# Storing the SwiGLU intermediate as two ready halves instead of splitting it where it is loaded

## The chip, the cores and the metric

The kernel runs on one core of a Trainium2 chip. The metric is the device time of one execution in microseconds, lower is better. The kernel is built by a tile framework: the program is written as Python calls on tiles, and a scheduler fixes the order in which each engine's queue gets its instructions.

## The reference, cut to what matters

Two layers, each a mixer and a SwiGLU channel mixer in sandwich norm, over 1024 tokens of width 1024 in float32. The change is in the two channel mixers (D_FF = 2816):

```
def sandwich(x, g_pre, g_post, fn):
    return x + rmsnorm(fn(rmsnorm(x, g_pre)), g_post)

def swiglu(h, w_gate, w_up, w_down):
    return (jax.nn.silu(h @ w_gate) * (h @ w_up)) @ w_down
```

## The kernel before

**Products in three parts.** Each float32 operand of a matmul is split into a rounded half hi (fp32r) and a remainder lo = x - hi. One product is three matmuls (`mm3`, L114): hi·hi, hi·lo and lo·hi, the fourth being left out. An operand is thus made ready by a cast (ScalarE) and a subtraction (VectorE or GpSimd).

**Seven products for eight.** The class `Ffn` computes both matrix products by a Strassen-Winograd scheme on 2x2 blocks: 7 products and a number of block sums.

**The up stage** (`up`, `pair`, L1168) has 11 iterations. Each makes seven products b1, b2, b5, b6, b3, b7, b4 of 24 matmuls of 512 columns, 168 in an iteration. The weights come in by SyncE (SP) as `raw` of 512 KB, ScalarE casts `wh` (L1121), GpSimd subtracts `wl` (L1123). VectorE adds the products out of PSUM (L1163, L1172), `emit` (L1141) applies silu on ScalarE (L1144) and multiplies by the up branch on VectorE (L1145), GpSimd makes four of the block sums in `store` (L1178). The seven blocks of h that an iteration makes, of 128 x 512 or 256 KB each, are stored to a DRAM buffer `h_s` (L1147, L1179).

**The down stage** (`down`, L1229) makes 42 products in passes over two (once one) of the 11 column blocks. `hraw` (L1244) loads a block pair of h (`hr`, 512 KB, L1246), `hx` casts it to `hh` (ScalarE, L1252) and subtracts `hl` (VectorE, L1253), each of 128 x 1024; four buffers of `hr`, `hh` and `hl`. The products go to banks named `psd`, in two loops over token blocks, `wide` and `slim`, and VectorE adds them to the accumulators `acc` (L1271). Block differences of the weights are made by `minus` (L1242). `end` runs the sandwich norm (L162 to L173) on finished rows; its loads are `r`, `gpost`, `gpre`.

**What else runs there.** In the up stage of layer 0, from `mid` on, the tables of the S5 layer are prepared by many small VectorE operations (`s5_prep`, from L583); they are independent of the FFN and run between its operations.

**Order.** All DMAs go through SP's queue in order, and each waits for the one eight places before it, since eight semaphores take turns. Every engine's queue is in order, so a waiting instruction holds all behind it. The split weights `wh` and `wl` go round a ring of three buffers, and of five between `K.more` and `K.less`; in layer 0's up stage the ring has three, in layer 1's five.

## Time and profile before

| | |
|---|---|
| median of 3 runs | 2328.96 us (2328.18 to 2329.32) |
| profiled execution | 2332.52 us, its span 2330.1 us, mean granted TensorE clock 0.968 |
| layer 0: up, down | about 493 to 961 us, 972 to 1195 us |
| layer 1: up, down | about 1627 to 2081 us, 2086 to 2318 us |

The profiled execution is 3.6 us above the median. Times in the rows are of that execution, counted from the span's start. "Idle before" and "releaser" tell how long an engine waited and what ended it; DMA share is the mean busy share of the 16 DMA engines.

### The profile page before, as it was taken

How to read it: one execution, taken by the hardware profiler on the slowest of the kernel's cores; microseconds unless marked ns; L12 is line 12 of the kernel's file. 1: busy time of each engine (PE TensorE's matmuls, PEld its weight loads, DVE VectorE, ACT ScalarE, POOL GpSimd, SP SyncE). 2: the span in 40 equal slices, each digit the busy share in tenths (PEclk: the TensorE clock that was granted, in tenths of full speed). 3: DMA queues.
4: the chain of work that ended last, by engine and by line, in shares of the span. 5: the costliest groups of instructions: out<-in, count | busy, mean ns of one | idle time of the engine just before them, and what ended most of it. 6: DMA issues, size and time to landing. Idle time of an engine off the chain costs nothing.

```text
span 2330.1 us, 27167 instructions
## 1 busy us (share of the span) xinstructions
PE 2157.9 (93%) x9684; PEld 1746.3 (75%) x9684; DVE 1594.9 (68%) x2175; ACT 945.2 (41%) x1413; POOL 1265.7 (54%) x740
## 2 busy tenths in 40 slices
PE   7999889898999999899969888999899999989987
PEld 5887677676788878687758767876688888878866
DVE  6859567689856865477884578656964444447788
ACT  5554555453222332333344346654532322234332
POOL 4997202134665556776644455421575656577674
PEclk9999999899999999899979999999999999999999
DMA  5234683243332343644542674324332323255354
GB/s 204 71 109 140 167 206 112 76 168 107 107 117 100 123 136 104 221 140 134 173 160 80 193 232 141 113 97 160 119 131 72 133 73 131 73 178 185 112 167 149
DMA packets 150662, 315.32 MB, mean 135 GB/s; under 512 B 20224, under 2 KB 43904, under 8 KB 150528
## 3 DMA queue, kind: packets, MB, share of 16 engines
q1 hardware_dynamic: 150528, 313.60, 41.4%
q8 instruction: 76, 1.25, 0.2%
q14 instruction: 58, 0.48, 0.1%
HBM read 214.39 MB, written 96.01 MB: 133 GB/s over the span
## 4 chain that ended last, share of the span: by engine, by line
PE 68%; DVE 16%; DMA 6%; issue 4%; ACT 3%; POOL 3%; SPq 0%; POOLq 0%; DVEq 0%; ACTq 0%
PE b L115 29%; PE psd L115 13%; PE psw L115 6%; PE psc L115 5%; PE psq L115 3%; PE po L115 2%; DVE hl L1253 2%; DVE acc L1271 2%; PE pss L1038 2%; PE trp L365 1%; POOL wl L1123 1%; DVE wt L1042 1%; PE pss L452 1%; DMA bm<-k_s 1%; PE psv L115 1%
## 5 line engine op out<-in xcount | busy, mean ns | idle before, releaser
L1123 POOL TENSOR_TENSOR wl<-raw,wh 128x1024 fp32r<-128x1024 f32 (+1 forms) x238 | 614.1, 2588 | 412.3 <-ACT wh L1121 399.7
L115 PE MATMUL b<-T,wh 128*128 128x512 f32 x1408 | 438.4, 392 | 2.2 <-DVE F L1172 2.2
L1121 ACT CAST wh<-raw 128x1024 fp32r<-128x1024 f32 (+1 forms) x238 | 241.9, 1023 | 433.0 <-PE b L115 251.7
L115 PE MATMUL b<-B,wh 128*128 128x512 f32 x1056 | 337.4, 400 | 15.0 <-DVE c L1163 10.5
L115 PEld LDWEIGHTS b<-T,wh 128*128 128x128 f32 x1408 | 263.8, 188 | 62.3 <-issue 2.8
L115 PE MATMUL b<-T,wl 128*128 128x512 f32 x704 | 276.4, 393 | 1.6 <-POOL wl L1123 1.6
L115 PE MATMUL psd<-wh,hh 128*128 128x512 f32 x616 | 240.6, 400 | 32.6 <-ACT hh L1252 18.9
L115 PEld LDWEIGHTS b<-B,wh 128*128 128x128 f32 x1056 | 203.0, 193 | 62.5 <-ACT B L1089 7.3
L115 PE MATMUL psd<-wl,hh 128*128 128x512 f32 x616 | 241.4, 396 | 0.0
L115 PE MATMUL psd<-wh,hl 128*128 128x512 f32 x616 | 235.2, 396 | 1.3 <-DVE hl L1253 1.3
L1271 DVE TENSOR_TENSOR acc<-acc,psd 128x512 f32<-128x512 f32 (+1 forms) x208 | 177.8, 884 | 60.1 <-PE psd L115 60.0
L115 PE MATMUL b<-B,wl 128*128 128x512 f32 x528 | 210.9, 400 | 3.6 <-POOL wl L1123 3.6
L115 PE MATMUL psw<-wh,jt 128*128 128x512 f32 x512 | 176.0, 410 | 16.0 <-ACT jt L488 9.3
L1172 DVE TENSOR_TENSOR p<-p,b 128x1024 f32<-128x1024 f32 (+1 forms) x88 | 83.5, 950 | 135.3 <-PE b L115 134.9
L1252 ACT CAST hh<-hr 128x1024 fp32r<-128x1024 f32 (+1 forms) x84 | 82.2, 979 | 223.8 <-PE psd L115 206.6
L115 PEld LDWEIGHTS psd<-wh,hh 128*128 128x128 f32 x616 | 117.2, 190 | 67.3 <-ACT hh L1252 23.9
L1253 DVE TENSOR_TENSOR hl<-hr,hh 128x1024 fp32r<-128x1024 f32 (+1 forms) x84 | 152.5, 1826 | 16.6 <-ACT hh L1252 16.6
L115 PEld LDWEIGHTS b<-T,wl 128*128 128x128 f32 x704 | 132.1, 188 | 32.7 <-POOL wl L1123 2.8
L91 POOL TENSOR_TENSOR wl<-raw,wh 128x1024 fp32r<-128x1024 f32 x48 | 122.2, 2558 | 58.4 <-ACT wh L89 58.4
L115 PEld LDWEIGHTS psd<-wh,hl 128*128 128x128 f32 x616 | 117.1, 190 | 28.9 <-DVE hl L1253 2.6
L115 PEld LDWEIGHTS psd<-wl,hh 128*128 128x128 f32 x616 | 117.5, 191 | 25.5
L1173 DVE TENSOR_TENSOR raw<-raw 128x1024 f32<-128x1024 f32 x66 | 106.7, 1617 | 41.3 <-POOL wl L1123 40.2
(386 smaller groups left out, 4314.4 us busy)
## 6 DMA issues: line engine op xcount, KB each, us to landing
raw<-in_l_gu_dram SPq DMA_DIRECT2D x96, 512.0 KB, 3.6
hr<-l_h_s SPq DMA_DIRECT2D x70, 512.0 KB, 4.1
raw<-in_l_dn_dram SPq DMA_DIRECT2D x48, 512.0 KB, 3.8
l_h_s<-F SPq DMA_DIRECT2D x66, 256.0 KB, 2.3
raw<-in_w_in_dram SPq DMA_DIRECT2D x27, 512.0 KB, 3.5
l_h_s<-c SPq DMA_DIRECT2D x44, 256.0 KB, 2.1
l_h_s<-p SPq DMA_DIRECT2D x44, 256.0 KB, 2.6
raw<-in_l_w_out_dram SPq DMA_DIRECT2D x16, 512.0 KB, 4.2
```

The source lines that it names most:

```text
L91: nc.gpsimd.tensor_tensor(lo, raw, hi.bitcast(F32), op=ALU.subtract)
L115: mm = lambda *t, **k: self.nc.tensor.matmul(*t, skip_group_check=go, **k)
L365: nc.tensor.transpose(tr[:, jj * P:(jj + 1) * P], Wt[:, offs[jj] + i * P:offs[jj] + (i + 1) * P], self.ident)
L452: nc.tensor.matmul(ps[:, b0:b0 + bw], Q[c][v][:, j * P:(j + 1) * P], M[c][:, b0:b0 + bw], start=v == 0, stop=v == 1)
L1038: nc.tensor.matmul(ps[:, ks], a[:, js], b[:, ks], start=first, stop=last)
L1121: nc.scalar.copy(hi[:, 0:n], r[:, 0:n])
L1123: nc.gpsimd.tensor_tensor(lo[:, 0:n], r[:, 0:n], hi[:, 0:n].bitcast(F32), op=ALU.subtract)
L1172: add = lambda o, a, b: v.tensor_tensor(o, a, b, op=ALU.add)
L1173: sub = lambda o, a, b: v.tensor_tensor(o, a, b, op=ALU.subtract)
L1252: nc.scalar.copy(hi[:, 0:n], r[:, 0:n])
L1253: v.tensor_tensor(lo[:, 0:n], r[:, 0:n], hi[:, 0:n].bitcast(F32), op=ALU.subtract)
L1271: v.tensor_tensor(dst, dst, ps, op=ALU.add)
```

## The change

The up stage makes the split: a new `put` casts each finished block to a tile `hs`, stores it, subtracts in place and stores the remainder, seven times in an iteration. `h_s` has both halves, twice the bytes. The down stage's `hx` loads both halves of a block pair in one DMA of 1 MB into a tile `h` (four buffers), which the matmuls read; the cast and the subtraction there go. Block 0 is put after GpSimd has read it, as the subtraction overwrites it. To make room, layer 1's up stage runs with the ring of three (`K.less`, `K.more`), and `s5_prep` has three big buffers for six and two of its small tiles in shared ones.

```diff
-        big = lambda n: pool.tile([P, 2, 9 * 16], F32, tag="pbig", name=n, bufs=6)
+        big = lambda n: pool.tile([P, 2, 9 * 16], F32, tag="pbig", name=n, bufs=3)
...
-        self.h_s = K.dr.tile([7, NF // 2, P, HALF], F32, name=p + "h_s")
+        self.h_s = K.dr.tile([7, NF // 2, P, 2, HALF], F32, name=p + "h_s")
...
-        if blk is not None:
-            nc.sync.dma_start(self.h_s[blk, i], g)
+
+    def put(self, blk, i, g):
+        nc = self.nc
+        hi = self.hs.tile([P, HALF], F32R, tag="hs", name="hs", bufs=2)
+        nc.scalar.copy(hi, g)
+        nc.sync.dma_start(self.h_s[blk, i, :, 0], hi.bitcast(F32))
+        nc.vector.tensor_tensor(g.bitcast(F32R), g, hi.bitcast(F32), op=ALU.subtract)
+        nc.sync.dma_start(self.h_s[blk, i, :, 1], g)
...
-        both(u4, 3)
-        store(c12[:, 1], c12[:, 0], u4[:, 0], ALU.add, 1)
-        store(u4[:, 1], c12[:, 1], c11[0], ALU.subtract, 5)
+        both(u4)
+        pool(c12[:, 1], c12[:, 0], u4[:, 0], ALU.add)
+        self.put(3, i, u4[:, 0])
+        pool(u4[:, 1], c12[:, 1], c11[0], ALU.subtract)
+        self.put(0, i, c11[0])
+        self.put(1, i, c12[:, 1])
...
-        both(p1, 2)
-        store(p1[:, 1], p1[:, 0], u4[:, 1], ALU.subtract, 4)
+        both(p1)
+        pool(p1[:, 1], p1[:, 0], u4[:, 1], ALU.subtract)
+        self.put(5, i, u4[:, 1])
+        self.put(2, i, p1[:, 0])
+        self.put(4, i, p1[:, 1])
...
-        def hraw(blk, i, n):
-            r = hp.tile([P, 2, HALF], F32, tag="hr", name="hr", bufs=4)
-            nc.sync.dma_start(r[:, 0:n], self.h_s[blk, i:i + n].rearrange("g p c -> p g c"))
+        def hx(blk, i, n):
+            r = hp.tile([P, 2, 2, HALF], F32R, tag="h", name="h", bufs=4)
+            nc.sync.dma_start(r[:, 0:n].bitcast(F32), self.h_s[blk, i:i + n].rearrange("g p s c -> p g s c"))
             return r
-
-        def hx(blk, i, n):
-            r = hraw(blk, i, n)
-            hi, lo = half("hh"), half("hl")
-            nc.scalar.copy(hi[:, 0:n], r[:, 0:n])
-            v.tensor_tensor(lo[:, 0:n], r[:, 0:n], hi[:, 0:n].bitcast(F32), op=ALU.subtract)
-            return hi, lo
...
+    K.less()
     G.up()
+    K.more(right)
```

What moves on the engines' queues, at the three places that matter most. In the rows, the tile left of the arrow is written, and the brackets name the semaphores waited for.

SP before, where layer 0 goes from up to down (`hr` are the loads of h, `r`, `gpost` and `gpre` those of the sandwich norm):

```order
L111 DMA gpost_9153<-in_l0_ffn_post_dram 128x1024 [waits DMAHW4_49,PE_49]
L111 DMA gpre_9155<-in_l1_mix_pre_dram 128x1024 [waits DMAHW5_49]
L1179 DMA l0_h_s_3857<-c11_7495 128x512 [waits Pool_49]
L162 DMA r_9151<-h1_84 128x1024 [waits DMAHW7_49]
L162 DMA r_9152<-h1_84 128x1024 [waits DMAHW0_49]
L162 DMA r_9268<-h1_84 128x1024 [waits DMAHW1_49]
L162 DMA r_9269<-h1_84 128x1024 [waits DMAHW2_49]
L1147 DMA l0_h_s_3857<-F0_3868 128x512 [waits DMAHW3_49,DVE_49]
L1246 DMA hr_7707<-l0_h_s_3857 128x2x512 [waits DMAHW4_49]
```

The same place in the change, where `h` are the loads and `hs` the stored casts:

```order
L1151 DMA l0_h_s_3857<-hs_7885 128x512 [waits DMAHW1_49,Activation_49]
L1153 DMA l0_h_s_3857<-c11_7775 128x512 [waits DMAHW2_49,DVE_49]
L1151 DMA l0_h_s_3857<-hs_7925 128x512 [waits DMAHW3_49,Activation_49]
L1257 DMA h_8015<-l0_h_s_3857 128x2x1024 [waits DMAHW4_49,PE_49]
L1151 DMA l0_h_s_3857<-hs_7931 128x512 [waits DMAHW5_49,Activation_49]
L1257 DMA h_8058<-l0_h_s_3857 128x2x1024 [waits DMAHW6_49,PE_49]
```

The first load of h no longer stands behind the six loads of the sandwich norm, which come 19 places after it, but behind a stored cast of the last iteration.

SP in the change, where layer 1 goes from up to down. The PE's first product reads h_16592, its second h_16733:

```order
L1257 DMA h_16592<-l1_h_s_12861 128x2x1024 [waits DMAHW1_49,PE_49]
L1151 DMA l1_h_s_12861<-hs_16511 128x512 [waits DMAHW2_49,Activation_49]
L1257 DMA h_16635<-l1_h_s_12861 128x2x1024 [waits DMAHW3_49,PE_49]
L1257 DMA h_16667<-l1_h_s_12861 128x2x1024 [waits DMAHW4_49]
L1257 DMA h_16695<-l1_h_s_12861 128x2x1024 [waits DMAHW5_49]
L1153 DMA l1_h_s_12861<-F0_12872 128x512 [waits DMAHW6_49,DVE_49]
L1151 DMA l1_h_s_12861<-hs_16516 128x512 [waits DMAHW7_49,Activation_49]
L1153 DMA l1_h_s_12861<-c11_16354 128x512 [waits DMAHW0_49,DVE_49]
L1153 DMA l1_h_s_12861<-F0_12872 128x512 [waits DMAHW1_49,DVE_49]
L1151 DMA l1_h_s_12861<-hs_16556 128x512 [waits DMAHW2_49,Activation_49]
L1153 DMA l1_h_s_12861<-F0_12872 128x512 [waits DMAHW3_49,DVE_49]
L1257 DMA h_16733<-l1_h_s_12861 128x2x1024 [waits DMAHW4_49,PE_49]
```

The fifth load takes the buffer of the first, and its wait for PE is for the last matmul of the first product. Before, the fifth load waited for VectorE's split of the first.

VectorE before, at the end of iteration 1 of layer 0's up stage (rows L531 to L537 are the S5 tables):

```order
L1172 TENSOR_TENSOR p1_4526<-p1_4526,b4_4939 128x512 [waits DVE_49,PE_49]
L533 TENSOR_TENSOR er_6002<-er_6002,et_6004 128x2x128 [waits DVE_49]
L1145 TENSOR_TENSOR F0_3868<-F0_3868 128x512 [waits Activation_49]
L535 TENSOR_TENSOR et_6004<-pi_5540,bb_5800 128x2x128 [waits DVE_49]
L1172 TENSOR_TENSOR p1_4526<-p1_4526,b4_4940 128x512 [waits PE_49]
```

The same place in the change:

```order
L1152 TENSOR_TENSOR c11_4577<-c11_4577,hs_4926 128x512 [waits Activation_49]
L1178 TENSOR_TENSOR p1_4525<-p1_4525,b4_4982 128x512 [waits DVE_49,PE_49]
L1145 TENSOR_TENSOR F0_3868<-F0_3868 128x512 [waits Activation_49]
L1178 TENSOR_TENSOR p1_4525<-p1_4525,b4_4983 128x512 [waits PE_49]
L1152 TENSOR_TENSOR F0_3868<-F0_3868,hs_4966 128x512 [waits Activation_49,Pool_49]
```

The subtractions of `put` (L1152) stand between the additions out of PSUM, where S5 operations stood. The addition of b4_4940 is VectorE's instruction 723 before, and that of b4_4983, the same one, 724 in the change: eight subtractions stand ahead of it, and seven or eight S5 operations have moved behind it. The first addition to F0 of iteration 0 was instruction 599 and is 641.

## Rows read from the trace of the kernel before

**Rows 1.** The page's part 4: the chain that ended last, shares by engine.

```profile
PE 68%; DVE 16%; DMA 6%; issue 4%; ACT 3%; POOL 3%; SPq 0%; POOLq 0%; DVEq 0%; ACTq 0%
```

**Rows 2.** Windows: length, then busy time (instructions) of PE, PEld, DVE, ACT, POOL; clock, DMA share, GB/s.

```profile
530.00:625.00 95.00, 87.45 (x350) 68.61 (x350) 90.55 (x182) 30.40 (x33) 53.46 (x24) 0.92 0.32 103
625.00:720.00 95.00, 95.00 (x418) 77.77 (x417) 51.45 (x49) 26.53 (x30) 57.47 (x28) 1.00 0.32 108
720.00:830.00 110.00, 108.91 (x493) 87.95 (x492) 93.29 (x122) 31.69 (x44) 58.06 (x29) 1.00 0.35 114
830.00:940.00 110.00, 110.00 (x482) 90.22 (x482) 59.01 (x61) 33.58 (x39) 70.10 (x35) 1.00 0.36 124
975.00:1100.00 125.00, 125.00 (x540) 102.12 (x539) 90.35 (x86) 46.67 (x54) 81.84 (x35) 0.99 0.45 148
1100.00:1145.00 45.00, 40.45 (x170) 30.87 (x169) 42.01 (x39) 15.40 (x16) 30.01 (x12) 1.00 0.59 191
1980.00:2080.00 100.00, 100.00 (x436) 81.51 (x435) 43.78 (x48) 27.67 (x31) 64.11 (x31) 1.00 0.27 92
2080.00:2090.00 10.00, 3.32 (x10) 1.91 (x9) 5.32 (x4) 3.63 (x4) 9.84 (x6) 0.69 0.98 331
2215.00:2260.00 45.00, 38.40 (x154) 29.21 (x153) 38.09 (x37) 15.97 (x17) 31.96 (x13) 0.96 0.55 178
2260.00:2320.00 60.00, 54.34 (x233) 42.86 (x231) 56.55 (x45) 19.88 (x27) 29.18 (x19) 1.00 0.40 134
```

**Rows 3.** The page's part 5: the cast and the subtraction of the down stages.

```profile
L1252 ACT CAST hh<-hr 128x1024 fp32r<-128x1024 f32 (+1 forms) x84 | 82.2, 979 | 223.8 <-PE psd L115 206.6
...
L1253 DVE TENSOR_TENSOR hl<-hr,hh 128x1024 fp32r<-128x1024 f32 (+1 forms) x84 | 152.5, 1826 | 16.6 <-ACT hh L1252 16.6
```

**Rows 4.** Groups by shape, VectorE, 720 to 940 us (layer 0, up).

```profile
L1145 DVE TENSOR_TENSOR F<-F 128x512 f32<-128x512 f32 x11 | 14.4, 1308 | 0.5
```

**Rows 5.** Groups by shape, VectorE, 1680 to 2080 us (layer 1, up).

```profile
L1145 DVE TENSOR_TENSOR F<-F 128x512 f32<-128x512 f32 x22 | 17.2, 783 | 2.0
```

**Rows 6.** Timeline of layer 0's turn from up to down: start, duration, engine, line, operation, idle before.

```profile
957.77 2.27 SPq L162 DMA_DIRECT2D r<-h  x4
...
962.44 3.51 SPq L1246 DMA_DIRECT2D hr<-l_h_s  x4
...
971.41 1.04 ACT L1252 CAST hh<-hr 128x1024 fp32r<-128x1024 f32 x1 [4.08 <-DMA hr<-l_h_s]
...
972.51 0.80 PE L115 MATMUL psd<-wh,hh 128*128 128x512 f32 x1 [11.61 <-ACT hh L1252]
```

**Rows 7.** The tile hr, 955 to 975 us, then 2078 to 2092 us: issue to landing.

```profile
DMA to landing us min/median/max: 6.8/9.1/9.8
...
DMA to landing us min/median/max: 5.0/6.0/8.2
```

**Rows 8.** Timeline of layer 1's turn from up to down.

```profile
2081.07 0.69 DVE L1172 TENSOR_TENSOR p<-p,b 128x512 f32<-128x512 f32 x1 [1.43 <-PE b L115]
...
2085.34 1.04 ACT L1252 CAST hh<-hr 128x1024 fp32r<-128x1024 f32 x1 [3.41 <-DMA hr<-l_h_s]
...
2086.41 6.63 DVE L1253 TENSOR_TENSOR hl<-hr,hh 128x1024 fp32r<-128x1024 f32 x2 [3.51 <-ACT hh L1252]
```

**Rows 9.** The chain of layer 0's last down pieces (1095 to 1225 us), one piece; start, duration.

```profile
1178.86 3.42 DVE hl L1253
```

**Rows 10.** The chain of layer 1's last down pieces, 2210 to 2320 us.

```profile
by line: PE psd L115 29.8%; DVE hl L1253 20.2%; DVE acc L1271 19.9%; issue 11.1%; DVE r L169 5.0%; DMA raw<-in_l_dn_dram 3.2%; DVE raw L1242 3.1%; ACT junk L106 2.3%; DVE m L168 2.2%; POOL rstd L97 2.1%; POOL rstd L98 1.0%; DVEq L1253 0.2%;
...
2259.35 4.38 DVE hl L1253 x2
...
2269.55 3.50 DMA raw<-in_l_dn_dram
...
2290.84 4.47 DVE hl L1253 x2
```

**Rows 11.** The page's part 6: the loads of h, their size and median time to landing.

```profile
hr<-l_h_s SPq DMA_DIRECT2D x70, 512.0 KB, 4.1
```

More of the change, by code (lines that the diff above doesn't have):

```diff
@@ L644, in s5_prep @@
         bb = sm("bb", (P, 2, 8, 16))
-        tb = sm("tb", (P, 8, 16))
+        tb = big("tb")[:, 0, 0:P].rearrange("p (g h) -> p g h", h=16)
         b16 = lambda t: o3(t).to_broadcast([P, 8, 16])
@@ L692, in s5_prep @@
             g = slice(4 * ch, 4 * ch + 4)
-            de = sm("de", (32, 4, 16))
+            de = big("de")[0:32, 0, 0:64].rearrange("p (g h) -> p g h", h=16)
             v.tensor_tensor(de, dsk[:, g].rearrange("p (g o) -> p g o", o=1).to_broadcast([32, 4, 16]), eye.rearrange("p (o h) -> p o h", o=1).to_broadcast([32, 4, 16]), op=ALU.mult)
@@ L702, in s5_prep @@
         yield
-        it = sm("tb", (P, P))
+        it = pool.tile([P, 4, P], F32, tag="pst", name="it")[:, 0, :]
         nc.gpsimd.iota(it, pattern=[[1, P]], base=0, channel_multiplier=0, allow_small_or_imprecise_dtypes=True)
@@ L708, in s5_prep @@
                 g = slice(4 * ch + 2 * h, 4 * ch + 2 * h + 2)
-                w = lambda n: pool.tile([P, 2, P], F32, tag="pbig", name=n, bufs=6)
+                w = lambda n: pool.tile([P, 2, P], F32, tag="pbig", name=n, bufs=3)
                 an, kk, co = w("an"), w("kk"), w("co")
@@ L1139, in duo, with emit @@
         return [self.K.pp.tile([P, HALF], F32, tag=tag, name=n) for _ in range(2)]
-    def emit(self, g, u, blk, i):
+    def emit(self, g, u):
         nc = self.nc
@@ L1163, in pre @@
                 nc.vector.tensor_tensor(c[k], self.p1[i][:, k], ps[k], op=ALU.add)
-            self.emit(c[0], c[1], 0, i)
+            self.emit(c[0], c[1])
             self.c11[i] = c
@@ L1173, in pair, with pool @@
         sub = lambda o, a, b: v.tensor_tensor(o, a, b, op=ALU.subtract)
-        both = lambda c, blk: self.emit(c[:, 0], c[:, 1], blk, i)
-        def store(o, x, y, op, blk):
+        both = lambda c: self.emit(c[:, 0], c[:, 1])
+        def pool(o, x, y, op):
             next(self.side, None)
             self.nc.gpsimd.tensor_tensor(o, x, y, op=op)
-            self.nc.sync.dma_start(self.h_s[blk, i], o)
         A11, A12 = [self.pre(i, k) if full else self.raw(self.gu[i, k]) for k in range(2)]
@@ L1200, in pair @@
         c11 = self.c11.pop(i)
-        self.emit(c12[:, 0], c12[:, 1], None, i)
-        store(c11[1], c11[0], c12[:, 0], ALU.subtract, 6)
+        both(c12)
+        pool(c11[1], c11[0], c12[:, 0], ALU.subtract)
+        self.put(6, i, c11[1])
         sub(A21, A11, A21)
@@ L1214, in pair @@
             add(p1[:, k], p1[:, k], b4[k])
-        both(p1, 2)
-        store(p1[:, 1], p1[:, 0], u4[:, 1], ALU.subtract, 4)
+        both(p1)
[3 more added lines that the diff above has]
+        self.put(4, i, p1[:, 1])
     def up(self, mid=None):
         with self.right("tc") as tc:
+            self.hs = tc
             self.x_sums(tc)
@@ L1235, in down @@
         seen = set()
-        half = lambda tag: hp.tile([P, 2, HALF], F32R, tag=tag, name=tag, bufs=4)
         def ld(blk, i, n):
@@ L1259, in mm @@
                 for g in range(n):
-                    K.mm3(ps, (H[0][:, g, ts], H[1][:, g, ts]), (W[0][:, g], W[1][:, g]), start and i + g == 0, (i, g) == (len(HW) - 1, n - 1), True)
+                    K.mm3(ps, (H[:, g, 0, ts], H[:, g, 1, ts]), (W[0][:, g], W[1][:, g]), start and i + g == 0, (i, g) == (len(HW) - 1, n - 1), True)
         def drain(k, lo, hi, ps):
```

## The prediction

> **What bounds the kernel now.** I read the chain of waits first: two thirds of the span is TensorE (PE), most of the rest VectorE [rows 1]. Then the windows, stage by stage [rows 2], since only where PE waits can something be won. At full speed PE does 436 matmuls in 100 us, 0.229 us each, and the down stages' middle (975 to 1100 us) is as full: 540 in 125 us. PE waits in four places that this change touches.
>
> - The start of layer 0's up stage, 530 to 625 us: 350 matmuls where 95 / 0.229 = 414 would go, so 64 x 0.229 = 15 us lost, with VectorE busy for 90.55 of 95 us.
> - The turn from up to down in layer 0: PE stands 11.61 us until the cast hh [rows 6]. The first hr is issued at 962.44, behind the loads r, lands with the others 9 us later [rows 7], and the cast takes 1 us more. In layer 1 the turn costs 5 to 9 us: the last addition is at 2081.07, hh starts at 2085.34, and the two subtractions hl run to 2093 [rows 8].
> - The end of layer 1's down stage, 2215 to 2320 us: 154 + 233 = 387 matmuls. 45 us and 58 us (the last psd is near 2318) would hold 449, so 62 x 0.229 = 14 us lost. In the chain there hl has 20.2% of 110 us, 22 us, in pieces such as 4.38 and 4.47 us [rows 10].
> - The same place in layer 0, 1100 to 1145 us: 170 for 196, 6 us lost; and after it the norm, whose chain holds an hl of 3.42 us [rows 9].
>
> All sums are against the profiled 2332.52 us, which lies 3.6 us above the median of 2328.96; I carry the difference over to the median.
>
> **What the change removes and adds.** It removes 84 casts (82.2 us of ScalarE) and 84 subtractions (152.5 us of VectorE) [rows 3] from stages where PE waits for them at the turns and the ends only. It adds 154 casts and 154 subtractions of 128x512 to the up stages, seven per iteration of 168 x 0.229 = 38.5 us. It also adds 154 stores of 256 KB and doubles the loads of h, 77 x 0.262 = 20.2 MB per layer each way. A subtraction has no row; the nearest is the multiplication L1145 of the same shape, 1308 ns in layer 0 [rows 4] and 783 ns in layer 1 [rows 5].
>
> *Layer 1, up: 0.* Seven subtractions are 5.5 us of VectorE per 38.5 us, where it is busy for 43.78 of 100 us [rows 2], and ScalarE at 28% has room for seven casts. With the ring of three, as in the order of the queues, a weight's cast still waits for a matmul at least 49 ahead of its use, 11 us; layer 0 runs so with PE full from 830 to 940 us. Upper end +8.
>
> *Layer 0, start: +5.* By the end of iteration 1 eight subtractions stand where S5 operations stood: 8 x (1.31 - 90.55/182) = 6.5 us of a busy engine. Iteration 0's first sum comes 42 places later, 21 us at 0.50 each, but VectorE has as much less to do from there to the end of iteration 1, so I take that as caught up. Ends 0 and +15.
>
> *Layer 0, iterations 5 to 8: +5.* From 720 to 830 us VectorE is busy for 93.29 of 110 us. 2.85 iterations bring 20 subtractions, 26 us at 1.31, into 16.7 us of room: 9 us over, of which the S5 work can hand some to its emptier neighbours (59.01 of 110 us). Ends 0 and +12.
>
> *Layer 0, the turn: -6.* The first h stands behind a stored cast and ahead of r, gpost and gpre, and nothing is split after it. It is 1 MB; issued at 961 it lands some 5 us later (4.1 us is the median of the 512 KB loads [rows 11]), so that PE starts at 966 or 967 for 972.5. Ends -8 and 0.
>
> *Layer 1, the turn: -3.5, then +8.* The first h lands at 2086, and PE runs without waiting for hl (full from 2089.8): -3.5, ends -5 and 0. But the second product reads the fifth load. Before, its buffer was free once VectorE had split the first; now it is free when PE has finished the first product, at 2086 + 5.5 = 2092. Ahead of it are four loads of 1 MB and the stores among them, 4.2 + 1.8 MB from 2081 on, 18 us at the 331 GB/s of 2080 to 2090 us [rows 2]; then its own 3.2 us. It lands near 2102 if nothing was moved earlier, at 2095 if the queue is empty: a wait of 3 to 10 us, and I take 8, since the DMA share there was 0.98 already.
>
> The Trainium skill (DMA: Bandwidth & Descriptors, Bandwidth) gives 6.15 us of busy time for a load of 1 MB, 341 GB/s; by that figure this wait is at least 6 us. The rate agrees with the 331 GB/s of the row; no run here has shown a load of this size.
>
> *Down stages, middle: +3.* Traffic rises from 148 GB/s by 20.2 MB in some 235 us, 86 GB/s, to 234. Followed through the semaphores, ten of the later loads may start only 37 matmuls (8.5 us) ahead of their use and two half-size ones 19 (4.4 us); the others have 31 or more. Single loads took 4.1 us, four abreast 6.8 to 9.8 [rows 7, 11]. Ends 0 and +16.
>
> *Ends of the down stages: -11 and -9.* Layer 1: of 14 us lost, 3 stay with the weights' load (3.50 us in the chain) and the additions acc. Ends -13 and -5. Layer 0: 5 of its 6 us, and 4 for the hl inside the norm's chain. Ends -13 and -3.
>
> Sum: 0 + 5 + 5 - 6 - 3.5 + 8 + 3 - 11 - 9 = **-8.5 us**: 2324 for the profiled execution, 2320.5 on the median. The ends, taken as independent, make about 15 us either way: 2306 to 2335 for this case.
>
> **Rivals.**
>
> - *The loads of h pace the down stages: slower.* The wait at buffers that only PE frees would return at every seventh product. If a 1 MB load needs 12 us from issue, ten places lose 3.5 us each: -8.5 - 3 + 35 = +23.5, 2352 us. It decides from 1.15 us beyond 8.5, that is at 9.65 us. For it: four abreast took 9.1. Against: the mean would be 234 GB/s where 331 was seen.
> - *VectorE becomes the bound of layer 0's up stage: slower.* From 530 to 940 us it is busy for 90.55 + 51.45 + 93.29 + 59.01 = 294 of 410 us [rows 2]. 77 subtractions at 1.31 bring 101, 395 in all: full but for 15 us. At 2.0 us each it is 448, 38 us over, in place of my 10: -18.5 + 38 = +19.5, 2348 us. The kernel is slower from 1.75 us each. For it: the same shape takes 783 ns in one layer and 1308 in the other, so what runs beside it matters; against it, that S5 operations can wait. The Trainium skill (GPSIMD Engine Reference, Key points) says that GpSimd shares its SBUF interfaces with VectorE and contends with VectorE instructions that have two SBUF inputs, as each of these subtractions has. The rows agree in direction, and by this rule the subtractions and wl would both stretch here.
> - *Little is won at the ends: no change.* hl was only the last to come there, and the additions (19.9% of the same chain) and the weights follow closely. With half of the -20: +10, so +1.5, 2330 us.
> - *The added work costs nothing in layer 0: faster still.* -18.5, 2310 us, if S5 operations always give way.
>
> **How the numbers follow.** Chances: my forecast 0.47, the loads 0.13, VectorE 0.13, little won 0.17, nothing lost 0.10. A measurement tells 0.2% from no change, 4.7 us. Within my forecast's range about two thirds are faster by more than that, a quarter within, the rest slower: 0.32, 0.11 and 0.04. To these go 0.10 faster from the last rival, and from the others 0.08 faster, 0.14 same and 0.21 slower. Together 0.50, 0.25 and 0.25. The range runs from 2300, below the last rival, to 2344, where it takes in half of the two slow ones.
>
> **What would show it.** PE's wait at 961 us ends 5 to 6 us sooner; after layer 1's first product a wait for a DMA of h of 3 to 10 us; no hl in the chains of the ends and over 430 matmuls in their last 105 us; L1152 at 0.8 us in layer 1 and 1.3 in layer 0, with fewer than 350 matmuls in the 95 us from 530. I am wrong if PE waits for h in the middle of the down stages, or if layer 0's up stage is over 15 us longer.

## The result and the profile after

| | median | runs | ratio to the kernel before |
|---|---|---|---|
| kernel before | 2329.14 us | 4 (2328.18 to 2330.14) | |
| changed kernel | 2341.15 us | 4 (2338.64 to 2346.61) | 1.0053, 95% interval 1.0039 to 1.0067 |

The change costs 12 us, 0.5%. That is inside the range of the prediction and on the wrong side of its forecast. The profiled execution took 2342.38 us, with a span of 2340.5 us.

The page of the changed kernel, parts 4 to 6 (columns as in [rows 1, 3, 11]):

```profile
PE 40%; DVE 7%; DMA 4%; POOL 3%; issue 3%; ACT 2%; SPq 0%; POOLq 0%; ACTq 0%; DVEq 0%
...
L115 PE MATMUL psd<-wh,h 128*128 128x512 f32 x1232 | 392.2, 398 | 33.4 <-DMA h<-l_h_s 27.1
...
h<-l_h_s SPq DMA_DIRECT2D x70, 1024.0 KB, 6.0
```

The rows hh and hl of [rows 3] are gone. TensorE's waits in front of psd are now for loads of h: 27.1 us in all, and 26.3 of them, as the timelines below show, are three waits at the two turns. (The shares of the chain add up to 59% here: it is followed back over that part of the span only. VectorE has 7 of these 59, 12%, where it had 16 of 100 in [rows 1].)

Stage by stage, in windows of the changed kernel (columns as in [rows 2]; the first four and that from 1980 us have the same times as there, the others are moved with the stage):

```profile
530.00:625.00 95.00, 82.64 (x336) 65.38 (x335) 93.90 (x174) 34.63 (x43) 42.84 (x21) 0.94 0.30 107
625.00:720.00 95.00, 94.36 (x414) 77.33 (x413) 72.52 (x65) 34.58 (x45) 61.99 (x28) 1.00 0.46 155
720.00:830.00 110.00, 107.45 (x485) 85.40 (x483) 99.69 (x117) 41.95 (x60) 60.87 (x30) 1.00 0.45 151
830.00:940.00 110.00, 102.71 (x428) 82.10 (x429) 92.46 (x107) 37.91 (x54) 59.76 (x29) 0.97 0.45 156
...
1000.00:1125.00 125.00, 119.92 (x512) 96.43 (x511) 55.82 (x64) 26.64 (x29) 79.47 (x39) 0.99 0.73 256
1125.00:1165.00 40.00, 38.92 (x169) 31.31 (x168) 24.90 (x27) 9.03 (x10) 25.57 (x12) 1.00 0.83 299
1980.00:2080.00 100.00, 100.00 (x439) 82.15 (x438) 74.66 (x66) 38.97 (x51) 64.54 (x30) 1.00 0.46 158
...
2105.00:2125.00 20.00, 12.22 (x33) 9.41 (x34) 10.62 (x8) 6.43 (x8) 10.50 (x6) 0.67 1.02 392
2225.00:2330.00 105.00, 104.66 (x455) 84.57 (x454) 72.07 (x75) 24.40 (x31) 61.60 (x36) 1.00 0.76 264
```

The end of layer 1 now holds 455 matmuls in 105 us where [rows 2] had 387, and the end of layer 0 is nearly full. Layer 0's up stage is worse in every window: from 830 to 940 us it makes 428 matmuls for 482.

Windows cannot be compared to the microsecond once the stages are moved. Every kernel of this study issues 9684 matmuls in the same order of products, so I compare the start of the k-th matmul with its start in the kernel before, and take differences over stretches. This table is worked out from the traces (us gained, minus, or lost, plus, against the kernel before; in brackets the numbers of the matmuls at either end; the last column holds the medians, taken from the timed runs):

```
                     layer 0                       layer 1
                     up       turn     down, norm  up       turn     rest
                     (2100-   (3916-   (4200-      (6888-   (8736-   (8904-
                     3916)    4200)    5040)       8736)    8904)    9683)    median us
changed kernel       +19.0    +6.5     -8.1        -2.5     +12.0    -13.7    2341.15
e1_ring5             +18.7    +7.7     -9.3        -3.5     +9.3     -13.8    2338.9
e2_last_sum_dve      +18.6    +0.9     -7.4        -3.0     +10.2    -13.9    2339.35
e3_layer1_only       -1.1     -0.6     +1.1        -1.8     +12.9    -13.0    2324.99
e4_no_sub_layer0     +6.2     -2.8     -6.1        -3.3     +11.9    -13.1    2322.46
e5_squeeze_only      +0.1     -0.8     +1.5        +0.9     -0.4     -0.2     2333.98
e6_hi_twice_layer0   +18.6    +3.9     -6.2        -3.1     +12.2    -13.9    2341.03
e7_late_only         +7.0     +11.9    -7.5        -3.4     +7.3     -3.5     2344.13
e8_layer1_late       -1.4     -0.8     +1.3        -6.2     +7.8     -3.2     2330.6
e9_act_queue         +20.2    +8.0     -7.1        -0.5     +8.7     -14.1    2345.81
e10_l1_ring6_act     -1.5     -0.5     +1.3        -1.2     +8.4     -13.5    2323.99
e11_l0_act_too       -0.7     -0.2     -0.2        -1.6     +10.4    -13.5    2322.82
e12_layer1_late_act  -1.4     -0.8     +1.3        -6.0     +10.9    -5.1     2334.68
```

Stages whose code is that of the kernel before come out within 1.5 us of zero: read the columns with that grain. The runs of one kernel lie up to 0.7% apart, and a profiled execution up to 6 us from the median of its kernel, so a row need not add up to its last column. The ratios below are to runs of the kernel before on the same chip.

Where the time went, then: layer 0's up stage loses 19.0 us, the turns 6.5 and 12.0; the rest of the two down stages gives back 8.1 and 13.7.

**Layer 0's up stage.** Windows of the changed kernel:

```profile
840.00:860.00 20.00, 17.96 (x78) 14.11 (x76) 16.56 (x29) 3.75 (x6) 4.81 (x4) 1.00 0.44 157
860.00:880.00 20.00, 14.88 (x54) 10.94 (x53) 19.97 (x26) 8.39 (x13) 11.55 (x6) 0.89 0.57 202
```

TensorE makes 54 matmuls where 87 would go, and VectorE is busy for 19.97 of 20 us. What VectorE waits for between 720 and 960 us in the changed kernel, then in the kernel before (total, times, longest):

```profile
DVE raw L1178 <- DMA raw<-in_l_gu_dram: 11.2, 5, 3.8
DVE p L1178 <- PE b L115: 7.1, 3, 3.1
...
DVE p L1172 <- PE b L115: 46.6, 13, 9.6
...
DVE raw L1172 <- DMA raw<-in_l_gu_dram: 6.1, 1, 6.1
```

and SyncE's queue from 720 to 930 us in the changed kernel:

```profile
SPq L1151 <- ACT hs L1150: 48.0, 15, 11.7
SPq L1115 <- POOL wl L1123: 16.1, 6, 5.3
SPq L1153 <- DVE c L1152: 10.7, 4, 3.8
SPq L1153 <- DVE p L1152: 10.7, 7, 4.1
```

VectorE's slack is gone: it waited 46.6 us for products b before, and 7.1 us now. SyncE's queue stands 48.0 us before stores of hs, and VectorE waits 11.2 us for weights that stand behind them, for 6.1 us before. Whether that way back through SyncE's queue carries the loss is asked in e6.

Most of the loss sits in one place. By the starts of the matmuls, 10.9 of the 19.0 us are lost at matmuls 3477 to 3564 (855 to 885 us), in iteration 8. VectorE is busy there for 30.1 of 30.7 us; over the same matmuls in the kernel before it was busy for 8.6 of 19.9. The last operation of the S5 tables comes at matmul 3567 (886 us); in the kernel before it came at matmul 3407 (831 us). So the tables' last operations now stand in VectorE's queue together with seven subtractions and the block sums of the weights (L1179).

**Layer 0's turn.** Timeline of the changed kernel:

```profile
972.78 4.73 POOL L1123 TENSOR_TENSOR wl<-raw,wh 128x1024 fp32r<-128x1024 f32 x2
...
977.47 1.29 POOL L1184 TENSOR_TENSOR c<-c,F 128x512 f32<-128x512 f32 x1
978.79 0.62 ACT L1150 CAST hs<-c 128x512 fp32r<-128x512 f32 x1 [9.82 <-POOL c L1184]
...
979.44 0.69 DVE L1152 TENSOR_TENSOR c<-c,hs 128x512 fp32r<-128x512 f32 x1 [4.61 <-ACT hs L1150]
980.05 1.21 DVE L1178 TENSOR_TENSOR F<-F,b 128x1024 f32<-128x1024 f32 x1
...
984.07 0.32 SPq L1151 DMA_DIRECT2D l_h_s<-hs  x1
...
984.48 0.39 SPq L1257 DMA_DIRECT2D h<-l_h_s  x1
...
990.06 0.76 PE L115 MATMUL psd<-wh,h 128*128 128x512 f32 x1 [9.55 <-DMA h<-l_h_s]
...
1014.20 0.72 PE L115 MATMUL psd<-wh,h 128*128 128x512 f32 x2 [3.62 <-ACT wh L1121]
```

The block sum c on GpSimd stands behind two subtractions wl; the cast hs waits for it, the subtraction on VectorE for the cast, and b7's addition stands behind that subtraction in VectorE's queue. The next stored cast follows from that addition, and the first load of h is behind its store in SyncE's queue: 984.48 for 962.44 [rows 6], 22 us later, of which the up stage explains 18. TensorE's wait itself is 9.55 us for 11.61. The load itself took 5.4 us from issue to landing. More is lost after it: from 990 to 1020 us the DMA engines are full (windows, share and GB/s last), and the wait of 3.62 us falls in that time.

```profile
990.00:1000.00 10.00, 9.94 (x33) 8.01 (x34) 4.32 (x5) 3.31 (x4) 3.75 (x3) 0.75 1.03 413
1000.00:1010.00 10.00, 8.76 (x39) 6.90 (x38) 2.52 (x3) 3.27 (x4) 1.69 (x1) 1.00 1.02 372
1010.00:1020.00 10.00, 6.16 (x19) 4.05 (x18) 1.22 (x1) 1.99 (x2) 5.78 (x3) 0.83 0.96 353
```

**Layer 1's turn** has the same chain and the wait that was forecast:

```profile
2094.97 0.69 DVE L1152 TENSOR_TENSOR c<-c,hs 128x512 fp32r<-128x512 f32 x1 [3.57 <-ACT hs L1150]
...
2100.02 0.39 SPq L1257 DMA_DIRECT2D h<-l_h_s  x1
...
2105.53 0.77 PE L115 MATMUL psd<-wh,h 128*128 128x512 f32 x1 [9.51 <-DMA h<-l_h_s]
...
2113.93 0.44 SPq L1257 DMA_DIRECT2D h<-l_h_s  x1
...
2121.15 0.76 PE L115 MATMUL psd<-wh,h 128*128 128x512 f32 x1 [7.25 <-DMA h<-l_h_s]
```

Not all of the turn's loss is waiting. Where two matmul starts lie more than 0.9 us apart, I count what exceeds 0.229 us as a wait: over matmuls 8736 to 8904 that is 17.1 us, and 7.2 in the kernel before. The other 2.2 of the 12.0 us are matmuls that start further apart while TensorE works. From 2105 to 2125 us it makes 33 in 12.22 us, 0.37 us each, at a mean granted clock of 0.67, that is partly at the lower of its two levels, 1.2 GHz; this comes after the two waits. In layer 0's turn it is 16.2 us of waits for 11.8, and 2.1 us of slower matmuls.

**Layer 1's end.** The chain of the changed kernel from 2225 to 2330 us, by line, answers to [rows 10]:

```profile
by line: PE psd L115 69.1%; POOL wl L1123 6.7%; DMA raw<-in_l_dn_dram 6.1%; issue 4.4%; DMA h<-l_h_s 4.2%; POOL raw L1253 2.3%; ACT junk L106 2.1%; ACT wh L1121 2.0%; DVE acc L1275 1.8%; POOL rstd L97 1.0%; POOL rstd L98 0.5%; DVEq L1253 0.
```

No hl, and acc at 1.8% for 19.9%: the additions had been late because VectorE was. TensorE has 69.1% for 29.8%.

### The profile page after: what moved, and what is told of

Its sections match the earlier page's. It is cut to its first block, busy times and chain, and to the rows that moved or that the text cites. A ratio compares the mean times of both kernels' runs of the same rounds, so it can differ in the third digit from the quotient of the medians.

```text
span 2340.5 us, 27672 instructions
## 1 busy us (share of the span) xinstructions
PE 2157.6 (92%) x9684; PEld 1746.5 (75%) x9684; DVE 1653.8 (71%) x2245; ACT 953.9 (41%) x1483; POOL 1250.1 (53%) x740
## 4 chain that ended last, share of the span: by engine, by line
PE 40%; DVE 7%; DMA 4%; POOL 3%; issue 3%; ACT 2%; SPq 0%; POOLq 0%; ACTq 0%; DVEq 0%
PE psd L115 16%; PE b L115 12%; PE psw L115 3%; PE pss L1038 2%; POOL wl L1123 1%; PE po L115 1%; PE psc L115 1%; DMA h<-l_h_s 1%; PE trp L365 1%; PE psu L115 1%; DMA raw<-in_l_dn_dram 1%; DVE wt L1042 1%; PE psr L115 1%; ACT junk L106 1%; DMA q_s<-sp 0%
## 5 line engine op out<-in xcount | busy, mean ns | idle before, releaser
L115 PE MATMUL psd<-wh,h 128*128 128x512 f32 x1232 | 392.2, 398 | 33.4 <-DMA h<-l_h_s 27.1
L115 PEld LDWEIGHTS psd<-wh,h 128*128 128x128 f32 x1232 | 235.2, 191 | 91.6 <-issue 21.4
L1275 DVE TENSOR_TENSOR acc<-acc,psd 128x1024 f32<-128x1024 f32 (+1 forms) x208 | 182.0, 890 | 153.0 <-PE psd L115 152.6
L115 PE MATMUL psd<-wl,h 128*128 128x512 f32 x616 | 244.5, 397 | 0.0
L1178 DVE TENSOR_TENSOR p<-p,b 128x1024 f32<-128x1024 f32 (+1 forms) x88 | 83.3, 948 | 99.3 <-PE b L115 96.3
L115 PEld LDWEIGHTS psd<-wl,h 128*128 128x128 f32 x616 | 117.6, 191 | 26.3 <-POOL wl L1123 0.4
L115 PEld LDWEIGHTS psw<-wh,jt 128*128 128x128 f32 x512 | 95.4, 189 | 41.4 <-ACT jt L488 16.8
L212 POOL TENSOR_TENSOR yconv<-yconv,cm 128x512 f32<-128x512 f32 x90 | 120.9, 1346 | 6.4 <-ACT cm L211 1.2
L115 PEld LDWEIGHTS b<-B,wl 128*128 128x128 f32 x528 | 100.5, 190 | 26.0 <-POOL wl L1123 4.9
L115 PE MATMUL psc<-xt,wh 128*128 128x512 f32 x352 | 112.7, 400 | 1.3 <-ACT xt L183 1.3
L217 DVE SCALAR_TENSOR_TENSOR psk<-cu,dww,psk 128x512 f32<-128x512 f32 x150 | 107.7, 751 | 2.6
```

Source lines behind the costliest of these rows:

```text
L115: mm = lambda *t, **k: self.nc.tensor.matmul(*t, skip_group_check=go, **k)
L212: nc.gpsimd.tensor_tensor(y, y, m, op=ALU.add)
L217: nc.vector.scalar_tensor_tensor(z, cu[:, o + k:o + k + HALF], w(k), z, op0=ALU.mult, op1=ALU.add)
L1178: add = lambda o, a, b: v.tensor_tensor(o, a, b, op=ALU.add)
L1275: v.tensor_tensor(dst, dst, ps, op=ALU.add)
```

## The experiments

The theory after the result had three parts. In layer 0's up stage the subtractions fill VectorE. At both turns the first load of h stands in SyncE's order behind stores that hang on GpSimd, ScalarE and VectorE. In layer 1 the fifth load waits for a buffer that only TensorE frees. Rivals: the added stores and the smaller pools; the time of the loads themselves in full DMA engines.

**e3_layer1_only: which layer loses?** Layer 0 uses a copy of the old class and the old pools, layer 1 the new class.

```diff
-    G = Ffn(K, "l1_", left, right)
+    G = Ffn2(K, "l1_", left, right)
```

> The change in layer 1 alone; layer 0, with the S5 tables, is the kernel before. Theory: the loss lies in layer 0 (matmul by matmul the changed kernel is 17 us behind where layer 1's up stage begins, and 10 us at the end), so layer 1 alone gains about 7 us: 2322. Rival: the layers are not separate, because a later layer 1 only gives back what waits have been moved about; then the time is 2329 within 2 us.

Measured: 2324.99 us, ratio 0.9977 (0.9966 to 0.9989). Layer 1 alone makes the kernel faster, by 4 us instead of the 7 expected: its end gives 13.0 us, its turn takes 12.9, and where the 4 us lie is below the grain of the table. The net loss of the whole change lies in layer 0, whose pools are those of before as well in this run.

**e4_no_sub_layer0: are the subtractions the cost?**

```diff
-        nc.vector.tensor_tensor(g.bitcast(F32R), g, hi.bitcast(F32), op=ALU.subtract)
+        if self.part:
+            nc.vector.tensor_tensor(g.bitcast(F32R), g, hi.bitcast(F32), op=ALU.subtract)
```

> The change with VectorE's subtraction left out in the up stage of layer 0 (77 of them; the second half stored is then the unsplit value). Casts, stores and loads stay. Theory: VectorE has too little room in layer 0's up stage beside the S5 tables; of the 18 us that the changed kernel is behind at the end of that stage at least 12 go, and the time is about 2329 or less. Rival: what is late there are DMAs: weights that stand behind the new stores and the S5 tables' stores in SP's queue, or waits for the three S5 buffers left of six; then less than 4 us go and the time stays over 2337.

Measured: 2322.46 us, ratio 0.9966 (0.995 to 0.9981). The up stage loses 6.2 us in place of 19.0, and the turn gains 2.8 in place of losing 6.5. The same stretch as above, in this run:

```profile
840.00:860.00 20.00, 17.09 (x73) 13.48 (x72) 19.20 (x24) 6.79 (x11) 12.90 (x7) 0.98 0.42 152
860.00:880.00 20.00, 18.71 (x76) 14.92 (x75) 13.26 (x19) 8.96 (x12) 10.94 (x6) 0.93 0.55 177
```

VectorE has room again from 860 us on (13.26 of 20), and TensorE makes 76 matmuls for 54. The subtractions carry 13 of the 19 us, and 9 us at the turn. What stays is lost at matmuls 3477 to 3564 (6.6 us), where the tables' last operations come in this run too.

**e6_hi_twice_layer0: or the waits of their stores?** The subtractions stay, but no store waits for them.

```diff
-        nc.sync.dma_start(self.h_s[blk, i, :, 1], g)
+        nc.sync.dma_start(self.h_s[blk, i, :, 1], g if self.part else hi.bitcast(F32))
```

> The change, but in layer 0 the second store of each block stores the cast tile again instead of the remainder; VectorE's 77 subtractions are still made (their results are used nowhere), with as many stores and bytes. Theory: the subtractions cost VectorE time, so layer 0's up stage stays as long as in the change (16 us or more behind at its end) and the kernel near 2340. Rival: the stores of the remainder hold SP's queue, and the weights behind them, until VectorE has come to the subtraction; then the stage gains 8 us or more and the kernel is at 2333 or less.

Measured: 2341.03 us, ratio 1.004 (1.0026 to 1.0053); the up stage loses 18.6 us as before. Its window shows VectorE as full and TensorE as empty:

```profile
860.00:880.00 20.00, 14.91 (x55) 11.20 (x56) 19.79 (x24) 8.11 (x13) 11.79 (x6) 0.91 0.42 151
```

What VectorE waits for between 720 and 960 us in this run:

```profile
DVE p L1179 <- PE b L115: 8.5, 5, 3.8
DVE raw L1179 <- DMA raw<-in_l_gu_dram: 5.1, 3, 3.0
```

It waits 5.1 us for weights, less than the 6.1 of the kernel before, and the stage loses the same. So it is VectorE's time that counts, and neither SyncE's wait for the remainders nor VectorE's own wait for weights. The stores of the casts, which wait for ScalarE, are still there in this run; they were not tried apart.

**e5_squeeze_only: or the smaller pools?** The kernel before with the three pools of `s5_prep` made smaller, as the change makes them (`pbig` 6 to 3, `tb`, `de` and `it` put into other tiles).

```diff
-        big = lambda n: pool.tile([P, 2, 9 * 16], F32, tag="pbig", name=n, bufs=6)
+        big = lambda n: pool.tile([P, 2, 9 * 16], F32, tag="pbig", name=n, bufs=3)
```

> The kernel before with one part of the change alone: three big buffers instead of six for the S5 tables, and two of their small tiles in shared ones. Theory: VectorE's subtractions are what fills layer 0's up stage, and this squeeze alone costs under 3 us: 2329 to 2332. Rival: the tables' operations wait for the DMAs that empty their buffers and hold VectorE and SP with them; then most of the 10 to 14 us that the changed kernel loses between 819 and 916 us appear here too: 2338 or more.

Measured: 2333.98 us, ratio 1.0008 (0.9997 to 1.0019): no change that this measurement can tell. Over layer 0's up stage 0.1 us, with 1.7 lost in its second half. The pools are not without effect, though: the tables' last operation comes at matmul 3531 instead of 3407, and 3.4 us are lost at matmuls 3477 to 3564, which other places give back. The smaller pools thus bring the tables into iteration 8, where the subtractions meet them. The subtractions with the larger pools were not tried, so how much of the 10.9 us needs both is open.

**e2_last_sum_dve: does GpSimd hold the turns?** In the last iteration block 6's sum goes to VectorE.

```diff
-        pool(c11[1], c11[0], c12[:, 0], ALU.subtract)
+        if i == NF // 2 - 1:
+            sub(c11[1], c11[0], c12[:, 0])
+        else:
+            pool(c11[1], c11[0], c12[:, 0], ALU.subtract)
```

> The change with one block sum (block 6 of the last iteration) on VectorE instead of GpSimd. Theory: in the changed kernel that sum stands behind the down stage's weights in GpSimd's queue, the cast waits for it, VectorE's subtraction for the cast, and the addition of b7 and with it the first load of h for the subtraction, 4 to 5 us late in both layers (issued at 984.48 us where the last matmul of the up stage ended near 980). Then the first load is issued 4 us sooner after the last up matmul, PE's waits of 9.55 and 9.51 us fall to 5 to 6 us, and the kernel to about 2333 us. Rival: the wait is the 1 MB load itself, which takes twice as long as one of 512 KB; then PE's waits stay over 8 us and the time within 2 us of 2341.

Measured: 2339.35 us, ratio 1.0039 (1.0025 to 1.0052). In layer 1 b7's addition comes at 2091.56 instead of 2095.58, but the first load only at 2097.30 instead of 2100.02 (this run is 1.2 us ahead of the changed kernel at matmul 8736), and TensorE's waits for it are 8.82 and 8.64 us in place of 9.55 and 9.51. The waits and the time are as the rival has them. GpSimd was one link; the stored cast behind it still holds the load. Layer 0's turn loses 0.9 us for 6.5, though hardly through the first wait: the later wait of 3.62 us did not come (1.5 at the most). Why it did not was not settled.

**e1_ring5: is the fifth load's wait the buffer?**

```diff
-            r = hp.tile([P, 2, 2, HALF], F32R, tag="h", name="h", bufs=4)
+            r = hp.tile([P, 2, 2, HALF], F32R, tag="h", name="h", bufs=5)
```

> The change with five buffers for the loaded h instead of four; the first four loads and all of layer 0's up stage stand as before in the queues. Theory: in layer 1 the fifth load waits for PE's first product, and the 7.25 us that PE stands before the second product (2121.15 us in the changed kernel's trace) come from that wait. Then this wait falls to under 2 us and the kernel to about 2334 us from 2341. Rival: the load is late because four loads of 1 MB and the stores fill the DMA engines; then it lands as late as before and the time stays within 2 us of 2341.

Measured: 2338.9 us, ratio 1.0039 (1.0024 to 1.0053). The fifth load is issued 8.5 us sooner, at 2105.43, and TensorE's wait for it falls only from 7.25 to 4.96 us. It landed 11.1 us after its issue, where it took 7.1 us in the changed kernel: issued sooner, it was slower. Neither theory nor rival fits in full: the buffer explains 2.3 us of the wait, and most of what it gave went to a longer load, beside DMA engines that are full (2105 to 2125 us at a share of 1.02 in the changed kernel's windows above).

**e9_act_queue: is the first load's wait SyncE's order?** The last iteration's stores go to ScalarE's queue.

```diff
-        nc.sync.dma_start(self.h_s[blk, i, :, 0], hi.bitcast(F32))
+        q = nc.scalar if i == NF // 2 - 1 else nc.sync
+        q.dma_start(self.h_s[blk, i, :, 0], hi.bitcast(F32))
         nc.vector.tensor_tensor(g.bitcast(F32R), g, hi.bitcast(F32), op=ALU.subtract)
-        nc.sync.dma_start(self.h_s[blk, i, :, 1], g)
+        q.dma_start(self.h_s[blk, i, :, 1], g)
```

> The whole change, with one difference: in the last iteration of each up stage both stored halves are issued from ScalarE's queue instead of SyncE's. The first load of h for the down stage then stands behind the last raw weights on SyncE's queue and ahead of no stored half; its buffer is free from that iteration's second product on. Theory (the first load waits in SyncE's order behind stores that hang on GpSimd, ScalarE and VectorE): TensorE's waits for h at the two turns fall from 9.55 and 9.51 us to 3 us or less, the stretch over layer 0's turn gives back about 6 us and that over layer 1's about 6 (the fifth load's 7.25 us is its own), time 2326 to 2332 us. Rival (the wait is the time of the load itself, beside the weights): both waits stay over 7 us, time 2338 us or more.

Measured: 2345.81 us, ratio 1.0063 (1.0044 to 1.0082). The waits did what the theory says, 4.05 us for 9.55 and 3.92 for 9.51, a little over the 3 us I gave; the time did not follow. Layer 0's turn in this run, TensorE's timeline, then a row of what ScalarE waits for from 975 to 1000 us:

```profile
986.76 0.77 PE L115 MATMUL psd<-wh,h 128*128 128x512 f32 x1 [4.05 <-DMA h<-l_h_s]
...
1000.88 0.79 PE L115 MATMUL psd<-wh,h 128*128 128x512 f32 x1 [6.93 <-ACT acc L1272]
```

```profile
ACT hs L1150 <- DMA l_h_s<-hs: 9.0, 3, 5.3
```

The casts hs, with two buffers, wait 9.0 us for their stores to land, and the copy of the first product out of PSUM stands behind them in ScalarE's queue; TensorE waits 6.93 us for that copy. Layer 0's turn loses 8.0 us, more than before. In layer 1 the turn loses 8.7 us for 12.0, with the fifth load's wait at 6.05 us. Order of the queue was the reason for more than half of the first wait, but taking it away brings the next one.

**e10_l1_ring6_act and e11_l0_act_too: layer 1 alone with both remedies.** e10 is e3 with six buffers of h and with e9's edit; e11 also issues layer 0's last stores (code of the kernel before) from ScalarE's queue:

```diff
-            self.nc.sync.dma_start(self.h_s[blk, i], o)
+            (self.nc.scalar if i == NF // 2 - 1 else self.nc.sync).dma_start(self.h_s[blk, i], o)
```

> The change in layer 1 alone (layer 0 as in the kernel before), with six h buffers there and the last iteration's stored halves issued from ScalarE's queue. The same edit without these two gave 2325 us, 4 us less than before, with TensorE's waits of 10.22 and 8.34 us at layer 1's turn. Theory (order of SyncE's queue for the first load, the buffer for the fifth): both waits together fall below 8 us, the stage's end keeps its gain of 13 us, time 2313 to 2319 us. Rival (at the turn the DMA engines are full, so that loads which start sooner only make each other and the weights later): the waits together stay over 12 us, time 2322 us or more.

> The run before this one, and layer 0 (code of the kernel before, one stored cast per block) also issues its last iteration's stores from ScalarE's queue, so that the first raw load of h stands ahead of them. Theory: TensorE's wait at layer 0's turn, 11.61 us in the kernel before, falls by 3 to 6 us, the kernel is 3 to 5 us below the run before it. Rival (the wait there is set by the load and by ScalarE's and VectorE's casts behind it, not by the place in the queue): the wait stays over 10 us, time within 2 us of the run before it.

Measured: e10 2323.99 us, ratio 0.9972 (0.9958 to 0.9986); e11 2322.82 us, ratio 0.9965 (0.9948 to 0.9982). In e10 the two waits are 3.88 and 5.20 us, 9.1 together, between what theory and rival gave, and a wait of 3.42 us for a weight has come in; the time is as the rival has it. The turn loses 8.4 us for 12.9. Windows of e10 at the turn:

```profile
2080.00:2090.00 10.00, 7.65 (x22) 6.11 (x23) 4.55 (x5) 2.41 (x4) 8.67 (x6) 0.66 1.02 399
2090.00:2105.00 15.00, 9.80 (x32) 7.54 (x31) 9.60 (x9) 4.43 (x6) 6.22 (x3) 0.77 1.04 412
```

For 25 us the DMA engines are full at 399 and 412 GB/s. e11's extra edit does nothing: TensorE's wait at layer 0's turn is 11.9 us there and 11.8 in e10. Its rival held. All three kernels with the change in layer 1 alone (e3, e10, e11) beat both the kernel before and the whole change; their intervals overlap, so none of them is shown to be the best.

**e7_late_only and e8_layer1_late: fewer halves.** Only iterations 7 to 10 store halves, which the late passes read; the early passes load the raw block and split it as before. e7 does so in both layers, e8 in layer 1 alone.

```diff
+        if i < self.late:
+            nc.sync.dma_start(self.h_s[blk, i], g)
+            return
+        i -= self.late
```

> The change for the last four column blocks alone (iterations 7 to 10), in both layers: earlier blocks are stored whole and split where they are loaded, as before; the last two passes of the down stages load both halves, with six buffers. Theory: the gain lies in the ends of the down stages (13 us in layer 1, 8 in layer 0) and the cost in layer 0's up stage and in the turns; this keeps the ends, four sevenths of the turn's cost falls away with the small loads, and layer 0's up stage loses under 8 us: 2312 to 2320. Rival: the gain at the ends came from loads that both turns had moved about; then the time is 2327 or more.

> The same late split in layer 1 alone; layer 0 is the kernel before. Theory: layer 1's end gains 13 us, its turn loses at most 5 where the whole change loses 12, its up stage nothing: 2317 to 2322, below layer 1 alone with the whole change (2325). Rival: the turn's loss comes from the stores of the last iteration, which are still doubled; then it is no better than 2325.

Measured: e7 2344.13 us, ratio 1.0052 (1.0039 to 1.0066); e8 2330.6 us, ratio 0.9998 (0.9984 to 1.0012). Both missed. Layer 0's up stage loses 7.0 us for 19.0, but its turn 11.9: the first raw load of h stands behind all stored halves of the last iteration, and TensorE waits 22.6 us for hh there. In e7 only iterations 7 to 10 have subtractions, and yet matmuls 3477 to 3564 lose 10.3 us: it is the meeting with the tables in iteration 8 that costs, more than the number of subtractions before it. The rest of layer 1 gives only 3.2 to 3.5 us: its end (from matmul 9240) still gives 8, but 4.8 us are lost in one place, matmuls 8940 to 8980, where TensorE waits for split weights (2.2 us in e8) and then works at a lower granted clock. Why the weights are late there I did not follow.

**e12_layer1_late_act: is what is left of layer 1's turn traffic?** e8 with the last iteration's stores in ScalarE's queue, so that the first pass reads half the bytes of h.

```diff
+        q = nc.scalar if i == NF // 2 - 1 else nc.sync
         i -= self.late
...
-        nc.sync.dma_start(self.h_t[blk, i, :, 0], hi.bitcast(F32))
+        q.dma_start(self.h_t[blk, i, :, 0], hi.bitcast(F32))
```

> Layer 1 alone, halves stored only for iterations 7 to 10 of the up stage, early passes of the down stage split their raw h blocks on loading as before, and the last iteration's stores are issued from ScalarE's queue. Against the run with six buffers and that queue (whole change in layer 1, 2324 us, 8.4 us lost over layer 1's turn) the first pass reads half the bytes of h. Theory (what is left of the turn's loss is traffic, the DMA engines being full there): over the turn, matmul 8736 to 8904, no more than 4 us are lost against the kernel before, and TensorE's longest wait there is 8 us or less; the end gains 4 to 10 us; time 2318 to 2324 us. Rival (the loss is the order of queue and engines, whichever bytes are read): 8 us or more are lost over the turn, time 2326 us or more.

Measured: 2334.68 us, ratio 1.0024 (1.001 to 1.0038). The turn loses 10.9 us, as the rival has it, 3.1 us more than in e8, from which only the queue of the last stores differs. The windows of this run:

```profile
2080.00:2090.00 10.00, 7.74 (x24) 5.61 (x24) 8.31 (x6) 5.13 (x6) 7.46 (x4) 0.71 0.48 174
2090.00:2105.00 15.00, 9.93 (x31) 7.64 (x32) 11.49 (x11) 6.93 (x8) 3.11 (x2) 0.77 0.86 306
```

The DMA engines are no longer full between 2080 and 2090 us (0.48 for 1.02), and TensorE is as empty: it now waits 10.08 and 4.71 us for the cast hh, that is for a load with a split behind it, on engines which still have the last iteration's casts and subtractions to do. The run does not separate the two cleanly: it takes bytes away and puts the split back. What it shows is that traffic alone is not the price of the turn.

**What stays open.** Of layer 1's turn 8 to 9 us remain after both waits were cut; it was not settled which of full DMA engines and late casts sets them when each is eased in turn. In e10, counted as above, 5.8 of the 8.4 us are waits and 2.7 are matmuls that start further apart (granted clock 0.66 and 0.77 in its windows), so not all of it is a wait to be cut. In e8 and e12 the up stage of layer 1 gains 6 us, more than in any other run; I did not follow that.

## Why the prediction was wrong, step by step

The forecast was -8.5 us on the profiled execution; the table adds up to +13.2 by the changed stages. (The profiled execution is 9.9 us longer; 2.5 us come back after the last matmul.)

- **Layer 0, start: +5. Right.** 4.9 us (matmuls 2100 to 2520), and 336 matmuls in the 95 us from 530 where fewer than 350 were asked; without the subtractions it is 1.4 (e4).
- **"Layer 0, iterations 5 to 8: +5", the largest error.** 14 us (matmuls 2520 to 3916), above the upper end of 12. The price of a subtraction was right: groups by shape on VectorE, 530 to 960 us of the changed kernel,

```profile
L1152 DVE TENSOR_TENSOR p<-p,hs 128x512 fp32r<-128x512 f32 x20 | 29.6, 1479 | 2.2 <-ACT hs L1150 2.1
L1152 DVE TENSOR_TENSOR F<-F,hs 128x512 fp32r<-128x512 f32 x30 | 28.2, 939 | 3.6 <-POOL F L1184 3.5
L1152 DVE TENSOR_TENSOR c<-c,hs 128x512 fp32r<-128x512 f32 x20 | 28.0, 1398 | 2.8 <-ACT hs L1150 2.8
```

  85.8 us for 70, 1.23 us each against 1.31. What failed is the sentence that the S5 work hands its excess to emptier neighbours. It did hand it on, and the neighbour filled: the stretch from 720 to 830 us, where I had counted 9 us over and taken 5, loses 2.6 us, and 10.9 us are lost in one place of the window from 830 to 940 us, which had 59.01 of 110 us busy before (both by the times of the kernel before). VectorE works in the order of its queue, and the tables' last operations stand there ahead of the weights' block sums and the additions out of PSUM. The sum also had no term for the smaller pools, which move the tables that far: without subtractions this place loses 3.4 us (e5) and 6.6 us (e4). This is near the second rival (VectorE the bound), which gave +19.5 for the kernel by a dearer subtraction; VectorE was the bound without the dearer price, and for some 30 us alone. Over the stage it was busy for 359 of the 410 us from 530 on, in place of the 395 that I added up.
- **"Layer 0, the turn: -6", wrong in sign.** +6.5. The step took the first load to be issued at 961, with the up stage's end, "behind a stored cast". It named the store and did not follow what that cast waits for. It hangs on GpSimd's queue, ScalarE and an in-order VectorE, and the load was issued some 4 us after the last up product (e2, e9) and 22 us later than before; from there it took 5.4 us, near the 5 forecast. The rest comes after the first product, while the DMA engines are full. That they are its cause is not shown. Without the subtractions the same turn gains 2.8 us (e4).
- **"Layer 1, the turn: -3.5, then +8": +12.0 for +4.5.** The fifth load's wait was 7.25 us, as forecast, though a fifth buffer takes only 2.3 of it away (e1), as the load is then slower. The -3.5 failed: the first load is late for the same reason as in layer 0, and cost 4.5 us (matmul 8760 at +19.1 after 8736 at +14.6).
- **Down stages, middle: +3.** 0.0 in layer 1 (8904 to 9240). In layer 0 TensorE does not wait for h either between 1025 and 1100 us. The first rival, loads of h that pace the down stages, did not come: their median from issue to landing is 6.0 us, under the 9.65 us where it decides. TensorE waited for loads of h in the turns.
- **Ends: -11 and -9. Right:** -13.7 and, with the middle, -8.1. The third rival (little won) is out: with VectorE free the additions came early as well.
- **Layer 1, up: 0. Right,** -2.5, although a subtraction cost 1.42 us there and not 0.78 (38.1 + 36.6 + 31.6 us for 75, groups by shape, 1640 to 2112 us).

By the sum: 9 us of the error are layer 0's up stage, 12.5 its turn, 7.5 layer 1's turn; the rest of the down stages gave back 5 more than forecast, layer 1's up stage 2.5. The signs that I had set for being wrong included an up stage of layer 0 over 15 us longer: it is 19.

The Trainium skill (DMA: Bandwidth & Descriptors, Specifications) gives 435 GB/s as the fabric ceiling of a core's DMA. The 413 GB/s of 990 to 1000 us here and the 412 of e10, at a share of 1.03 and 1.04, stand close under it, and well over the 331 GB/s from which I had priced the turn. The turn was not faster for it: at 392 GB/s, 7.8 MB went through from 2105 to 2125 us alone, where I had counted 6.0 MB ahead of the fifth load.

## What to carry to other kernels

A mean busy share hides a stretch where the engine is full: VectorE had 294 of 410 us busy before the change and 359 after it, and 10.9 us were lost where it had 30.1 of 30.7. Price added work by the fullest 20 us of the stage, and look where the work that gives way ends up, for a queue runs in order. When a load is moved behind a store, follow that store back to the last engine that it hangs on, and every instruction which stands behind it on the way. Work moved out of a stage's end was won there in full, as forecast. It was lost again where two stages meet, for there the queues, the buffers and the DMA engines were at their limit at once. The change was worth keeping in the one layer whose up stage had room, for 0.2%.
